# Identity matmuls in planned idle stretches of TensorE: a hybrid recurrent backbone on one core

## The chip, the cores and the metric

The kernel runs on 1 core of one Trainium2 chip, in one launch. The metric is device time in microseconds (us) of the whole program. PE is TensorE, DVE is VectorE, ACT is ScalarE, POOL is GpSimd, SP is SyncE, which here issues the DMAs.

## The reference

Four layers of one trunk over 512 tokens (256 context, 256 latent) of width 1024, in float32. Each layer mixes tokens by two parallel recurrences and then applies a gated feed-forward:

```
hg, rw, gt = split(modulate(rms_norm(x)) @ w_in[l])        # 1024 -> 6528 columns
o_hg = hgrn2_branch(hg)      # 4 heads, gated linear recurrence, both directions
o_rw = rwkv7_branch(rw)      # 8 heads, S = S*w + sa b^T + v k^T, both directions
m = sigmoid(g_hg) * (o_hg @ proj_a) + sigmoid(g_rw) * (o_rw @ proj_b)
x = x + gate * rms_norm(m @ w_out)
x = x + gate2 * rms_norm((silu(gt) * up) @ w2)             # hidden width 2816
```

The shifts, scales and gates come from a conditioning vector through `ada_w` (6144 columns a layer). The recurrences of the latent tokens start from the final states of the context. In the last layer the context gives only those states.

## The kernel before

Activations stand transposed, 128 channels by 512 tokens a tile. Each large product is made of three matmuls on high and low parts of weights and activations: a weight block lands in `wr`, ACT copies its high part to `wh`, DVE or POOL subtracts to get `wl`, and PE adds `wl*hh`, `wh*hh` and `wh*hl` into a PSUM bank `p_ps`. Small products use the banks `s_ps`, `g_ps` and `c_ps`.

The RWKV branch runs as four pairs of heads, in chunks of 64 tokens. `rw_pair` prepares a pair, `rw_solve` inverts small triangles on DVE (tiles `XS`, `S`), and `rw_chain` walks over 8 chunks with its products in one bank, `c_ps`. A step of the walk goes over the engines in turn: 4 matmuls `c_ps<-UV,SC`; ACT copies the result to `S`; 4 matmuls with the inverse; ACT copies to `UV`; 4 matmuls `c_ps<-UV,BKT`; then 6 updates on DVE, 4 of `UV` and 2 of `S`, each of which reads `c_ps`; then the next step.

No instruction is issued where the source calls it. All calls are recorded as nodes of a graph (`Plan.add`), `Plan.schedule` puts them in an order for each engine by assumed costs, ranks and lags between engines, and `Plan.emit` issues them in the order of the planned times. The plan has its own picture of PE's clock: in stretches that it believes slow it doubles PE's costs, and what it believes changes the order of real work. When the calls are issued, the framework adds the semaphore waits that reads and writes of a tile need, for the tile as a whole.

The first work of the program is `ada_first`: 32 matmuls of `ada_w` rows into `g_ps`, as the DMAs land, in two groups of 16; then four transposes by the identity `ident`; beside them the first norm (squares on ACT into `fn`, of which there are three buffers, summed on PE by `ones` into `s_ps`). `ident` is loaded by a DMA that the plan puts 25th on SP's queue.

Of the kernel before, what the change touches and what calls it, by code (L numbers as in the profile page):

```python
# [2 lines left out]

# [6 lines left out]
F32 = mybir.dt.float32  # L10
F32R = mybir.dt.float32r
U8 = mybir.dt.uint8
AF = mybir.ActivationFunctionType
# [3 lines left out]
P = 128  # L17
# [12 lines left out]
C = 64  # L30
# [40 lines left out]
        ('pe', True): 30, ('act', True): 0, ('vec', True): 30, ('pool', True): 0, ('dma', True): 0}  # L71
MAXLOOK = 200
WINDOW, COLD = 4096 / 1.2, (0.39, 0.87)


def bias_of(bias, kind):
    return bias[kind[1]].get(kind[0], 0.0) if kind else 0.0


def isc(kind):  # L80
    return kind is not None and kind[0] == "C"


class Node:
# [4 lines left out]
    def __init__(self, engs, calls, preds, costs, load, kind):  # L89
        self.engs, self.calls, self.preds, self.costs, self.load, self.kind = engs, calls, preds, costs, load, kind  # L90


class Plan:
# [4 lines left out]

    def __init__(self, nc, tc):
        self.tc, self.nodes, self.tiles, self.tags, self.gang, self.kind = tc, [], {}, {}, None, None  # L100
        self.share = 1.0
        self.eng = dict(zip(self.ENG, (nc.tensor, nc.scalar, nc.vector, nc.gpsimd, nc.sync)))
        for name in self.ENG:
            setattr(self, name, Recorder(self, (name,)))
        self.any = Recorder(self, ("vec", "pool"))
# [137 lines left out]
    def schedule(self):  # L243
        nodes = self.nodes
        N = len(nodes)
        succ = [[] for _ in range(N)]
        need = [0] * N
        for i, x in enumerate(nodes):
            need[i] = len(x.preds)
            for p in x.preds:  # L250
                succ[p].append(i)
        rank = [0.0] * N
        for i in range(N - 1, -1, -1):
            x = nodes[i]
            lag = self.LAG.get(x.engs[0])
            m = 0.0
            for s in succ[i]:
                v = rank[s] + (lag[nodes[s].engs[0]] if lag else DMA_LAG + x.load)
                if v > m:
                    m = v  # L260
            rank[i] = m + x.costs[0]
        rank = [r + bias_of(BIAS, x.kind) for r, x in zip(rank, nodes)]
        ready = {e: [] for e in self.ENG}
        later = {e: [] for e in self.ENG}
        free = {e: 0.0 for e in self.ENG}
        when = [0.0] * N
        on = [None] * N
        bus = 0.0
        edge, busy, cold = WINDOW, 0.0, True
        tail = 1e9  # L270

        def release(i):
            for e in nodes[i].engs:
                heapq.heappush(later[e], (when[i], i))

        for i in range(N):
            if not need[i]:
                release(i)
        order = []
        while len(order) < N:  # L280
            best = None
            for e in self.ENG:
                while ready[e] and on[ready[e][0][1]]:
                    heapq.heappop(ready[e])
                while later[e] and on[later[e][0][1]]:
                    heapq.heappop(later[e])
                if ready[e]:
                    t = free[e]
                elif later[e]:
                    t = max(free[e], later[e][0][0])  # L290
                else:
                    continue
                if best is None or t < best[0]:
                    best = (t, e)
            t, e = best
            while later[e] and later[e][0][0] <= t:
                _, i = heapq.heappop(later[e])
                if not on[i]:
                    heapq.heappush(ready[e], (-rank[i], i))
            if ready[e] and later[e] and later[e][0][0] <= t + MAXLOOK:  # L300
                r0 = -ready[e][0][0]
                m = min((x for x in later[e] if x[0] <= t + MAXLOOK and rank[x[1]] > r0 + 2000.0 and not on[x[1]]
                         and x[0] <= t + LOOK[e, isc(nodes[x[1]].kind)]), default=None)
                if m is not None and m[0] + 1e-6 < t + nodes[ready[e][0][1]].costs[0]:
                    free[e] = m[0]
                    continue
            _, i = heapq.heappop(ready[e])
            x = nodes[i]
            on[i] = e
            c = x.costs[x.engs.index(e)]  # L310
            if e == "pe":
                if t <= free[e]:
                    c += max(0.0, x.head - tail)
                tail = x.tail
                while t >= edge:
                    cold = busy < (COLD[1] if cold else COLD[0]) * WINDOW
                    busy = max(0.0, free[e] - edge) if free[e] > edge else 0.0
                    edge += WINDOW
                if cold:
                    c *= 2.0  # L320
                busy += (min(t + c, edge) - t) * x.load
            end = t + c
            free[e] = end
            order.append((t, i))
            if e == "dma":
                bus = max(bus, t) + x.load
            for s in succ[i]:
                r = bus + DMA_LAG if e == "dma" else end + self.LAG[e][nodes[s].engs[0]]
                if r > when[s]:
                    when[s] = r  # L330
                need[s] -= 1
                if not need[s]:
                    release(s)
        order.sort()
        self.when, self.on = order, on
        return max(free.values())
# [17 lines left out]
def body(ctx, tc, xT, cc, ada_w, w_in, rw_lo, rw_g2, proj_a, proj_b, w_out, ffn_w1, ffn_w2,  # L354
         vecs, lbl, c_id, c_bo, c_sc, c_hg, c_sh, out, depth=4):
    nc = tc.nc
    plan = Plan(nc, tc)
    vec, act, pool, pe, dma = plan.vec, plan.act, plan.pool, plan.pe, plan.dma
# [6 lines left out]
    pss = ctx.enter_context(tc.tile_pool(name="pss", bufs=1, space=PSUM))  # L365
# [9 lines left out]
    def const(ap, dt=F32, name=None):  # L375
        t = plan.tile(cst, list(ap.shape), dt, None, 1, name)
        dma.dma_start(t, ap)
        return t

    ident = const(c_id, name="ident")  # L380
# [14 lines left out]
    vec.memset(onef, 1.0)  # L395
    vec.tensor_copy(ones, onef)

    def sps(tag="s"):
        return plan.tile(pss, [P, 512], F32, tag, PSB[tag], tag + "_ps")

    hgf = st("SS", [P, 6, C])
# [119 lines left out]
    def proj(src, nk, c0, xh, xl, t0, place=None):  # L521

        ps = sps("p")
        if place:
            ws = weights(src, nk, c0, place)
            for c, a, b in halves(t0):
                for k, (wh, wl) in enumerate(ws):
                    mm3(ps[:, a:b], wh, wl, xh[k][:, a:b], xl[k][:, a:b], k == 0, k == nk - 1)
            return ps
        for k0 in range(0, nk, KB):  # L530
            n = min(KB, nk - k0)
            wh, wl = load_split(src, k0, n, c0, P)
            for k in range(n):
                kk = k0 + k
                mm3(ps[:, t0:T], wh[:, k, :], wl[:, k, :], xh[kk][:, t0:T], xl[kk][:, t0:T],
                    kk == 0, kk == nk - 1)
        return ps
# [204 lines left out]
    hd = (slice(0, C), slice(C, P))  # L742

    def layer(l, pm, xs, xd, hh, hl):
        last = l == depth - 1
# [285 lines left out]
        def rw_chain(p):  # L1031
# [12 lines left out]
            for s in range(NCH):  # L1044
                ps = sps("c")
# [53 lines left out]
                with plan.together(0.75):  # L1099
                    for x in steps:  # L1100
                        st_, i, d, n = x
                        for h in range(2):
                            po = ps[hd[h], 384 + i * C:384 + (i + 1) * C]
                            if st_:
                                w, a = S[hd[h], d, n % 4, :], ARt[hd[h], d, n, 1, :]
                            else:
                                w, a = UV[:, d, n, h, :], SC[:, d, n, h, C:P]
                            pe.matmul(po, w, a[:, ::-1] if d else a, start=x == steps[0], stop=fin[i] == x,
                                      skip_group_check=True)
                st_ = ns[1] - ns[0]  # L1110
                act.activation(y.rearrange("p (n c) -> p n c", c=C)[:, ns[0]:ns[1] + 1:st_],
                               ps[:, 384:512].rearrange("p (n c) -> p n c", c=C), AF.Copy)
                flags["chain", p] = s
                yield 1

# [2 lines left out]
            ps = sps()  # L1118
# [6 lines left out]
            ps = sps()  # L1125
# [7 lines left out]
            ps = sps()  # L1133
# [184 lines left out]
        while run:  # L1318
# [8 lines left out]
            try:  # L1327
                x = next(r[3])
# [99 lines left out]
        if not last:  # L1428
            ada_to(l + 1, 2)
        h = norms(xs, t0, (pr[:, 5], lambda j: proj(ffn_w2[l], NF, j * P, gh, gl, t0),  # L1430
                           tail(ffn_w2[l], NF, gh, gl, spot), NK if last else NK - NTL[1]),
                  None if last else (pms[l + 1]["pr"][:, 0], pms[l + 1]["pr"][:, 1]))
# [31 lines left out]
    h = norms(xs, 0, pre=(pms[0]["pr"][:, 0], pms[0]["pr"][:, 1]))  # L1464
    for l in range(depth):
        ada["end"] = l + 1
        xs, xd, h = layer(l, pms[l], xs, xd, *h)
# [57 lines left out]
```

## Time and profile before

| what | value |
|---|---|
| median of 3 runs | 4313.35 us (4310.06 to 4324.89) |
| profiled execution, its own time | 4312.55 us |
| its span, first to last instruction | 4310.8 us |
| PE busy | 3855.0 us, 89% |
| DVE busy | 3309.3 us, 77% |
| ACT busy | 2149.9 us, 50% |
| mean granted clock of PE | 0.932 of 2.4 GHz |

The granted clock takes two levels, 1.2 and 2.4 GHz; a mean of a stretch says how much of it was at either. Idle before an instruction is idle time of its engine, with what ended it. A float32 matmul stands in the trace as two passes, so 4 matmuls are 8 rows there; a transpose is one.

### The profile page before, as it was taken

The page shows a single profiled execution, that of the slowest core. Times are in us where ns is not written, and L with a number is a line of the kernel's source. Part 1 is how long each engine was busy: PE and PEld are TensorE (multiplying, and loading weights), DVE is VectorE, ACT ScalarE, POOL GpSimd, SP SyncE. Part 2 cuts the span into 40 slices and gives each one's busy share as a digit, 9 for nine tenths or more (in the row PEclk, how much of TensorE's full clock was granted, in tenths as well). Part 3 has the DMA queues.
Part 4 walks back from the last instruction along what each step waited for, and adds up shares of the span by engine and source line. Part 5 has one row for each costly group of instructions (what it writes and reads, how often), then busy time and mean ns, then how long its engine had stood idle before and what let it go on. Part 6 is the DMA issues. An engine that isn't in the chain of part 4 may idle for free.

```text
span 4310.8 us, 71511 instructions
## 1 busy us (share of the span) xinstructions
PE 3855.0 (89%) x26290; PEld 3058.9 (71%) x26290; DVE 3309.3 (77%) x5764; ACT 2149.9 (50%) x4234; POOL 1890.7 (44%) x1617
## 2 busy tenths in 40 slices
PE   7889998899988998999999889899899997788898
PEld 4666666777776666677777766677777775567798
DVE  5989979999179899668753898987676379988676
ACT  4556653433255566544333555565433255566564
POOL 1343444455433444464554243454455433244332
PEclk8889899999998898999999989899999998788999
DMA  4111137466321111363543212116354331112555
GB/s 150 57 53 48 52 122 217 138 182 177 91 85 52 59 50 55 122 186 115 159 123 107 64 38 63 43 56 221 108 164 140 108 102 45 41 51 63 170 151 160
DMA packets 661407, 451.02 MB, mean 105 GB/s; under 512 B 28224, under 2 KB 584256, under 8 KB 661056
## 3 DMA queue, kind: packets, MB, share of 16 engines
q1 hardware_dynamic: 661056, 446.44, 34.7%
q8 instruction: 207, 3.39, 0.3%
q14 instruction: 144, 1.18, 0.1%
HBM read 416.98 MB, written 29.36 MB: 104 GB/s over the span
## 4 chain that ended last, share of the span: by engine, by line
PE 42%; DVE 19%; issue 10%; POOL 5%; ACT 2%; DMA 1%; POOLq 0%; SPq 0%; DVEq 0%; ACTq 0%
PE p_ps L343 32%; POOL wl L343 4%; PE s_ps L343 4%; DVE XS L343 4%; PE c_ps L343 3%; PE g_ps L343 2%; DVE wl L343 2%; DVE S L343 2%; DVE X8b L343 1%; DVE AR L343 1%; DVE hX L343 1%; DVE UV L343 1%; DVE X8a L343 1%; DVE BK L343 1%; DVE X4c L343 1%
## 5 line engine op out<-in xcount | busy, mean ns | idle before, releaser
L343 PE MATMUL p_ps<-hh,wl 128*128 128x512 f32 (+1 forms) x2784 | 1091.0, 397 | 107.0 <-DVE wl L343 53.5
L343 PE MATMUL p_ps<-hh,wh 128*128 128x512 f32 (+1 forms) x2784 | 1073.9, 390 | 0.0
L343 PE MATMUL p_ps<-hl,wh 128*128 128x512 f32 (+1 forms) x2784 | 1066.2, 389 | 0.0
L343 ACT ACTIVATE wh<-wr 128x512 fp32r<-128x512 f32 x986 | 611.0, 622 | 860.8 <-PE p_ps L343 684.4
L343 POOL TENSOR_TENSOR wl<-wr,wh 128x512 fp32r<-128x512 f32 x487 | 674.3, 1392 | 746.9 <-ACT wh L343 517.0
L343 PEld LDWEIGHTS p_ps<-hh,wl 128*128 128x128 f32 x2784 | 543.7, 196 | 245.9 <-POOL wl L343 77.0
L343 PEld LDWEIGHTS p_ps<-hl,wh 128*128 128x128 f32 x2784 | 541.8, 195 | 97.6 <-issue 7.2
L343 PEld LDWEIGHTS p_ps<-hh,wh 128*128 128x128 f32 x2784 | 543.6, 196 | 90.7 <-issue 4.9
L343 DVE TENSOR_TENSOR wl<-wr,wh 128x512 fp32r<-128x512 f32 (+1 forms) x499 | 377.6, 762 | 99.6 <-ACT wh L343 89.9
L343 POOL TENSOR_SCALAR fn<-fn 128x512 f32<-128x512 f32 (+1 forms) x152 | 236.4, 1555 | 246.1 <-ACT fn L343 220.0
L343 POOL TENSOR_SCALAR S0P<-S,pcs 128x64 f32<-128x64 f32 x192 | 151.4, 802 | 316.8 <-DVE S L343 316.2
L343 DVE TENSOR_TENSOR fn<-fn,p_ps 128x512 f32<-128x512 f32 (+1 forms) x208 | 127.7, 615 | 162.0 <-ACT fn L343 81.2
L343 ACT ACTIVATE fn<-fn 128x512 f32<-128x512 f32 (+1 forms) x304 | 174.5, 575 | 103.2 <-POOL fn L343 98.8
L343 POOL TENSOR_TENSOR HB<-HB,HA 128x512 f32<-128x512 f32 x112 | 157.7, 1408 | 155.2 <-ACT hY L343 153.2
L343 DVE TENSOR_TENSOR XS<-XS,S 64x30 f32<-64x30 f32 (+14 forms) x480 | 203.9, 425 | 11.7
L343 DVE TENSOR_TENSOR S<-XS 64x30 f32<-64x30 f32 (+14 forms) x480 | 193.2, 402 | 11.6
L343 POOL COPY SC<-XS 64x256 f32<-64x256 f32 x128 | 67.6, 528 | 263.1 <-DVE SC L343 250.3
L343 POOL TENSOR_TENSOR HA<-HA 128x512 f32<-128x512 f32 x112 | 144.2, 1287 | 11.4 <-ACT hX L343 5.0
L343 PE MATMUL p_ps<-SC,wh 128*128 128x512 f32 (+1 forms) x440 | 144.2, 361 | 0.0
L343 DVE SCALAR_TENSOR_TENSOR UV<-c_ps,pcs,S0P 64x64 f32<-64x64 f32 x384 | 108.6, 283 | 36.7 <-PE c_ps L343 26.6
L343 ACT ACTIVATE fn<-p_ps 128x512 f32<-128x512 f32 (+1 forms) x217 | 112.2, 518 | 42.9 <-PE p_ps L343 23.6
L343 ACT ACTIVATE hY<-HB 128x512 f32<-128x512 f32 x128 | 85.0, 664 | 89.2 <-PE g_ps L343 74.5
(478 smaller groups left out, 8761.7 us busy)
## 6 DMA issues: line engine op xcount, KB each, us to landing
wr<-ffn_w SPq DMA_DIRECT2D x512, 256.0 KB, 3.1
wr<-w_in SPq DMA_DIRECT2D x408, 256.0 KB, 2.9
hq<-ada_w SPq DMA_DIRECT2D x242, 256.0 KB, 3.0
PB<-ada_w SPq DMA_DIRECT2D x110, 256.0 KB, 2.8
wr<-w_out SPq DMA_DIRECT2D x64, 256.0 KB, 3.0
gts<-fn SPq DMA_DIRECT2D x48, 256.0 KB, 2.4
wr<-proj_a SPq DMA_DIRECT2D x32, 256.0 KB, 3.9
wr<-proj_b SPq DMA_DIRECT2D x32, 256.0 KB, 3.6
```

The source lines that it names most:

```text
L343: getattr(self.eng[self.on[i]], name)(*args, **kw)
```

## The change

A chain's bank `c_ps` was a new tile in each step; it is now one tile, `cbank`, for the whole program. The outputs of the chain that stood in its columns 384 to 511 move to 128 to 255. The freed columns take filler matmuls, identity times identity, 128x128 in float32. They are put in by `schedule`: where PE's next node would start at least 300 ns after PE is free, and the plan's running measure of PE's use is under 0.85, fillers of assumed 216 ns are placed from the free time on, as long as 300 ns are left. Their time counts in the plan's picture of the clock. The fillers are not nodes with predecessors or successors. The first may be placed once the plan has issued (not landed) the DMA of `ident`.

```
+FILL, FMIN, FUSE = 216.0, 300.0, 0.85
...
+                f = free[e]
+                while f >= since and t - f >= FMIN and use < FUSE:
+                    turn(f)
+                    d = 2.0 * FILL if cold else FILL
+                    nodes.append(Node(("pe",), [self.filler], set(), [FILL], 1.0, None))
+                    on.append("pe")
+                    order.append((f, len(nodes) - 1))
+                    fills += 1
+                    spent(f, d, 1.0)
+                    f += d
+                turn(t)
...
+            if i == self.needs:
+                since = end
...
+    cbank = plan.tile(pss, [P, 512], F32, None, 1, "c_ps")
+    plan.filler = ("matmul", (cbank[:, 384:512], ident, ident), dict(start=True, stop=True))
+    plan.needs = plan.tiles[ident.tensor.name][0][0][0]
...
-                            po = ps[hd[h], 384 + i * C:384 + (i + 1) * C]
+                            po = ps[hd[h], 128 + i * C:128 + (i + 1) * C]
```

The built program has 297 fillers in 78 places: 31 before the first `p_ps` matmul, 93 in the rest of the first three layers, and 173 in the last layer. The order of real work changes too: taking the fillers out, 12388 of 20460 matmul rows of PE stand at the same position; the rest, all four layers' mixing stages among it, is rearranged, and the feed-forward stages are mostly as they were.

The first place is PE's start, before. `g_ps<-SC,ep` are the first matmuls of `ada_first`; the names in brackets are the semaphores an instruction waits for, `DMAHW0` to `DMAHW7` those of DMAs in turn.

```order
L343 MATMUL g_ps<-SC,ep 32x512 [waits DMAHW4_49]
L343 MATMUL g_ps<-SC,ep 32x512 [waits DMAHW5_49]
L343 MATMUL g_ps<-SC,ep 32x512 [waits DMAHW6_49]
L343 MATMUL g_ps<-SC,ep 32x512 [waits DMAHW7_49]
L343 MATMUL g_ps<-SC,ep 32x512 [waits DMAHW0_49]
...
L343 MATMUL g_ps<-BKT,ep 32x512 [waits DMAHW1_49]
L343 MATMUL s_ps<-fn,ones 128x256 [waits Activation_49] x2
L343 MATMUL g_ps<-UV,ep 32x512 [waits DMAHW1_49]
```

The same stretch of PE after the change.

```order
L373 MATMUL g_ps<-SC,ep 32x512 [waits DMAHW4_49]
L373 MATMUL c_ps<-ident 128x128 [waits DMAHW6_49]
L373 MATMUL g_ps<-SC,ep 32x512 [waits DMAHW5_49]
L373 MATMUL g_ps<-SC,ep 32x512
L373 MATMUL g_ps<-SC,ep 32x512 [waits DMAHW7_49]
...
L373 MATMUL c_ps<-ident 128x128 x2
...
L373 MATMUL c_ps<-ident 128x128 x12
L373 MATMUL s_ps<-fn,ones 128x256 [waits Activation_49] x2
L373 MATMUL c_ps<-ident 128x128 x13
L373 MATMUL g_ps<-UV,ep 32x512 [waits DMAHW1_49]
```

A filler now stands fifth on PE and waits for the DMA of `ident`; the two later matmuls whose data come by earlier DMAs of the same semaphore need no wait of their own any more. 27 further fillers stand between it and the second group of `g_ps`. SP's first 41 rows are as they were.

The second place is the first step of the third chain in the last layer, on PE, before.

```order
L343 MATMUL s_ps<-wd_5213,BK 128x512 [waits PE_49]
L343 MATMUL c_ps<-UV,BKT 64x64 [waits Activation_49]
L343 MATMUL c_ps<-UV,BKT 64x64 x3
L343 MATMUL s_ps<-ad_5219,BK 128x512 [waits PE_49]
L343 MATMUL s_ps<-wd_5213,BK 128x512
L343 MATMUL s_ps<-ad_5219,BK 128x512
L343 MATMUL c_ps<-UV,SC 64x64 [waits DVE_49,PE_49]
```

The same step on PE after.

```order
L373 MATMUL s_ps<-ad_5124,BK 128x512
L373 MATMUL c_ps<-UV,BKT 64x64 [waits Activation_49]
L373 MATMUL c_ps<-UV,BKT 64x64 x3
L373 MATMUL c_ps<-ident 128x128 x2
L373 MATMUL c_ps<-ident 128x128 [waits DVE_49] x6
L373 MATMUL c_ps<-UV,SC 64x64 x4
```

Eight fillers stand between the two products of the chain, and six of them each wait for a DVE instruction.

The third place is DVE's updates in that step, before.

```order
L343 TENSOR_TENSOR hX<-hX,og 128x256 [waits DVE_49]
L343 TENSOR_SCALAR UV<-c_ps,pcs 64x64 [waits PE_49,Activation_49]
L343 TENSOR_SCALAR UV<-c_ps,pcs 64x64 x3
L343 TENSOR_SCALAR S<-c_ps,pcs 128x64 x2
L343 TENSOR_TENSOR X8b<-X8a 64x8x64 [waits Activation_49]
```

The same updates after.

```order
L373 TENSOR_TENSOR X8a<-X8a,X8b 128x512
L373 TENSOR_SCALAR UV<-c_ps,pcs 64x64 [waits PE_49,Activation_49]
L373 TENSOR_SCALAR UV<-c_ps,pcs 64x64 [waits PE_49] x3
L373 TENSOR_SCALAR S<-c_ps,pcs 128x64 [waits PE_49] x2
L373 TENSOR_TENSOR X8b<-X8a 64x8x64 [waits DVE_49]
```

Before, the first update waits for PE and the other five follow it. After, each of the six waits for PE: a filler writes the tile that the updates read, so the filler waits for the update before it, and the update behind it waits for the filler. Over the whole program 25 DVE updates, all in the last layer, wait in this way for a filler that itself waits for a DVE update; 8 other DVE updates and 12 ACT copies wait for a run of fillers (45 in all) that follows the matmuls they read; and the other 15 fillers that wait for ACT (11) or DVE (4) stand ahead of further real work of the chain.

## Rows read from the trace of the kernel before

**Rows 1.** The cores' view: span and mean granted clock.

```profile
core 0: 4310.8 us, clock 0.932
```

**Rows 2.** The page's chain that ended last: share of the span by engine.

```profile
PE 42%; DVE 19%; issue 10%; POOL 5%; ACT 2%; DMA 1%; POOLq 0%; SPq 0%; DVEq 0%; ACTq 0%
```

**Rows 3.** Timeline of PE, 4 to 59 us: start, us, instruction, [idle before <-releaser].

```profile
4.86 7.08 PE L343 MATMUL g_ps<-SC,ep 128*32 128x512 f32 x16 [4.86 <-DVE ep L343]
14.48 3.04 PE L343 MATMUL g_ps<-BKT,ep 128*32 128x512 f32 x8
22.86 2.07 PE L343 MATMUL s_ps<-fn,ones 128*128 128x256 f32 x4 [5.34 <-ACT fn L343]
35.04 2.56 PE L343 MATMUL g_ps<-UV,ep 128*32 128x512 f32 x4 [10.11 <-DMA UV<-ada_w]
...
38.52 0.62 PE L343 MATMUL g_ps<-X8a,ep 128*32 128x512 f32 x2
...
40.77 1.36 PE L343 MATMUL g_ps<-X4c,ep 128*32 128x512 f32 x4
49.21 1.11 PE L343 MATMUL g_ps<-ident,fn 128*128 128x128 f32 x4 [7.07 <-ACT fn L343]
...
58.02 0.50 PE L343 MATMUL p_ps<-hh,BKT 128*128 128x256 f32 x2 [1.98 <-ACT hh L343]
```

**Rows 4.** SP's issue of `ident`, and DMA issues: count, size, us to landing.

```profile
25.16 0.33 SPq L343 DMA_DIRECT2D ident<-c_id  x1
ident<-c_id SPq DMA_DIRECT2D x1, 64.0 KB, 4.4
```

**Rows 5.** Timeline of ACT, 24 to 49 us.

```profile
24.12 0.42 ACT L343 ACTIVATE fn<-XS 128x256 f32<-128x256 f32 x1 [0.70 <-PE s_ps L343]
30.76 0.63 ACT L343 ACTIVATE SC<-wr 128x512 fp32r<-128x512 f32 x1 [6.22 <-DMA wr<-w_in]
...
48.57 0.58 ACT L343 ACTIVATE fn<-g_ps 128x512 f32<-128x512 f32 x1
```

**Rows 6.** Windows of mixing in the last three layers, and two inside the last.

```profile
core 0: us, PE busy (x) PEld busy (x) DVE busy (x) ACT busy (x) POOL busy (x), PEclk, DMA share, GB/s
1235.00:1816.00 581.00, 516.78 (x4296) 392.34 (x4295) 508.82 (x976) 333.82 (x670) 237.63 (x228) 0.90 0.20 60
2376.00:2943.00 567.00, 505.25 (x4272) 383.12 (x4271) 494.19 (x971) 330.83 (x666) 229.19 (x225) 0.92 0.19 57
3505.00:4023.00 518.00, 435.15 (x3837) 350.06 (x3836) 460.50 (x938) 306.90 (x665) 215.42 (x225) 0.87 0.20 59
3720.00:3780.00 60.00, 38.76 (x373) 31.62 (x374) 54.81 (x112) 26.09 (x52) 14.09 (x19) 0.63 0.10 29
3860.00:3900.00 40.00, 26.71 (x259) 21.78 (x260) 37.09 (x81) 16.23 (x37) 12.77 (x21) 0.64 0.08 24
```

**Rows 7.** Chain that ended last in 3505 to 4023 us, by line.

```profile
by line: PE p_ps L343 22.2%; DVE XS L343 9.2%; PE s_ps L343 7.9%; PE c_ps L343 6.5%; issue 6.4%; DVE wl L343 6.1%; DVE S L343 5.8%; DVE AR L343 4.8%; DVE X8b L343 3.9%; PE g_ps L343 3.4%; DVE UV L343 2.9%; DVE hX L343 2.4%; DVE X8a L343 2.3
```

**Rows 8.** Timeline of PE and DVE, third chain's first step in the last layer.

```profile
3862.29 0.45 PE L343 MATMUL c_ps<-UV,BKT 128*64 128x64 f32 x8
3862.86 1.18 DVE L343 TENSOR_SCALAR UV<-c_ps,pcs 64x64 f32<-64x64 f32 x4 [1.12 <-PE c_ps L343]
3864.05 0.48 DVE L343 TENSOR_SCALAR S<-c_ps,pcs 128x64 f32<-128x64 f32 x2
3864.68 0.65 PE L343 MATMUL c_ps<-UV,SC 128*64 128x64 f32 x8 [0.85 <-DVE S L343]
```

**Rows 9.** 128x128 matmuls by the identity: tile's view (min/median/max ns), groups by form.

```profile
L343 PE MATMUL g_ps<-ident,fn x4: 421/421/475, 49.2 to 49.9; 128*128 128x128 f32 x4
L343 PE MATMUL s_ps<-ident,BK 128*128 128x128 f32 x128 | 21.0, 286 | 5.6 <-DVE SC L343 5.5
```

**Rows 10.** DVE's reads of `c_ps`, whole program: idle time before them, by what ended it.

```profile
  PE c_ps L343: 33.2, 35
```

More of the change, by code (lines that the diff above doesn't have):

```diff
@@ L1 @@
 import heapq
+import math
 from contextlib import ExitStack, contextmanager
@@ L100, in __init__ @@
         self.tc, self.nodes, self.tiles, self.tags, self.gang, self.kind = tc, [], {}, {}, None, None
-        self.share = 1.0
+        self.share, self.filler, self.needs = 1.0, None, None
         self.eng = dict(zip(self.ENG, (nc.tensor, nc.scalar, nc.vector, nc.gpsimd, nc.sync)))
@@ L270, in schedule, with turn, spent @@
         tail = 1e9
+        use, last, fills, since = 0.0, 0.0, 0, 1e18
+        def turn(t):
+            nonlocal edge, busy, cold, use, last
+            while t >= edge:
+                cold = busy < (COLD[1] if cold else COLD[0]) * WINDOW
+                busy = max(0.0, last - edge) if last > edge else 0.0
+                edge += WINDOW
+            if t > last:
+                use *= math.exp((last - t) / WINDOW)
+                last = t
+        def spent(t, c, load):
+            nonlocal busy, use, last
+            busy += (min(t + c, edge) - t) * load
+            w = math.exp(-c / WINDOW)
+            use = use * w + load * (1.0 - w)
+            last = t + c
         def release(i):
@@ L279, in schedule @@
         order = []
-        while len(order) < N:
+        while len(order) < N + fills:
             best = None
@@ L314, in schedule @@
                 tail = x.tail
[L315 to L318, printed above, removed]
+                f = free[e]
[9 more added lines that the diff above has]
+                turn(t)
                 if cold:
                     c *= 2.0
-                busy += (min(t + c, edge) - t) * x.load
+                spent(t, c, x.load)
             end = t + c
@@ L396, in body @@
     vec.tensor_copy(ones, onef)
+    cbank = plan.tile(pss, [P, 512], F32, None, 1, "c_ps")
+    plan.filler = ("matmul", (cbank[:, 384:512], ident, ident), dict(start=True, stop=True))
+    plan.needs = plan.tiles[ident.tensor.name][0][0][0]
     def sps(tag="s"):
+        if tag == "c":
+            return cbank
         return plan.tile(pss, [P, 512], F32, tag, PSB[tag], tag + "_ps")
@@ L1111, in rw_chain @@
                 act.activation(y.rearrange("p (n c) -> p n c", c=C)[:, ns[0]:ns[1] + 1:st_],
-                               ps[:, 384:512].rearrange("p (n c) -> p n c", c=C), AF.Copy)
+                               ps[:, 128:256].rearrange("p (n c) -> p n c", c=C), AF.Copy)
                 flags["chain", p] = s
```

## The prediction

> **What bounds the kernel now.** I read the cores' view first: a span of 4310.8 us at a mean granted clock of 0.932 [rows 1]. With two levels, 1.0 and 0.5, that is (1 - 0.932) / 0.5 = 13.6% of the span at the lower one, some 586 us. The chain that ended last lies 42% on PE and 19% on DVE [rows 2]. If the slow time were spread evenly over the chain's PE work, a full clock throughout would give back at most 0.42 x 586 / 2 = 123 us. So the clock is worth something; the question is what 297 fillers reach of it, and what they hold up.
>
> Next I read the windows. In the last layer's mixing, 3505 to 4023 us, DVE is busy 460.5 of 518 us and PE 435.2, at a mean clock of 0.87; in the two slowest stretches, 3720 to 3780 and 3860 to 3900, the clock is 0.63 and 0.64, PE is busy 38.8 of 60 and 26.7 of 40 us, but DVE 54.8 and 37.1 [rows 6]. DVE sets the pace there, and PE is slow because it is waiting. The chain by line says the same: in that mixing PE's four PSUM lines hold 22.2 + 7.9 + 6.5 + 3.4 = 40%, DVE's lines most of the rest [rows 7]. Of the fillers, 173 of 297 stand in this layer, and 31 at the start of the program. I work out these two places and bound the rest.
>
> **The start.** In the trace the first g_ps matmuls run from 4.9 us as their data land, and the first group ends near 17.5 us [rows 3]. After the change the fifth instruction on PE waits for ident, which SP issues at 25.16 us and which lands 4.4 us later, at 29.6 us [rows 4]. SP's order ahead of it is unchanged and waits for nothing on PE, so that landing stays. PE stands from some 8 us to 29.6 us. Then it has to run what it had done before: 12 matmuls of g_ps, 24 passes. A pass costs 0.139 us where nothing holds it (26 passes from 38.52 to 42.13 us [rows 3]), so 3.3 us. With them stand 28 fillers; a pass of 128 columns at the lower clock comes every (1.11 - 0.42) / 3 = 0.23 us [rows 3, 9], a filler is two, so 0.46 us, or 0.23 us at the full clock: 6.4 us. The norm's two matmuls take 2.07 us at the lower clock [rows 3], about 1 us at the full one. Together 10.7 us at the full clock. PE has been idle, so I let the first 4.5 us run at half speed (before, PE ran slowly from 35.04 to about 38.5 us [rows 3]): 29.6 + 10.7 + 2.25 = 42.6 us, where the second group of g_ps began at 35.04; its 32 passes, now unhindered, take 4.5 us and end at 47.1 us instead of 42.1: 5 us late.
>
> The other path is ACT's. Its fourth square, at 24.12 us, waits for the first norm matmul on PE to free a buffer [rows 5]; that matmul now comes at about 39 us. Behind the square in ACT's queue stand the weight copies that began at 30.76 us and, as the last of them all, the copy of g_ps at 48.57 us [rows 5]. They start near 39.5 us, 8.8 us late. Some waits of theirs for DMAs shrink, since the data have landed meanwhile; I take 2 to 3 us off, which leaves 6 to 7. The transposes that begin at 49.21 us [rows 3], and everything after them, wait for that copy. I take +6.5 us, with ends of +4 (all of ACT's lag recovered but PE's part) and +9 (none recovered). Nothing later can hide it: the whole first layer hangs on this norm.
>
> **The chain of the last layer.** Before, the 4 + 2 updates of a step run back to back on DVE, 1.18 + 0.48 us, and the next matmul starts 0.15 us after the last (3864.53 to 3864.68 us); the first starts 0.12 us after PE's matmuls end (3862.74 to 3862.86 us) [rows 8]. With a filler between two updates DVE pays, for each, 0.15 us to PE, one filler, and 0.12 us back. No filler is in the trace; the nearest rows are the identity matmuls of one pass, 0.286 us at mostly full clock and 0.421 at the lower [rows 9], to which the second pass adds 0.115 or 0.23. So a round trip is 0.27 + 0.40 = 0.67 us, or 0.27 + 0.65 = 0.92. There are 25: 17 to 23 us. I take 0.75 us each, 19 us. Queued behind the waiting update are all of DVE's other instructions, and DVE is the engine that is 89% busy in this mixing, so no cover is left; the lower end is still 5 us, if many updates stand where DVE would have waited for PE anyhow. In the trace DVE waited for c_ps 35 times, 33.2 us in all, in the 112 steps of the program [rows 10].
>
> By the same rows a third of the readers that wait for a run of fillers would be there in time to feel it: 20 readers, 2.25 fillers each, 0.23 to 0.46 us a filler; 20 / 3 x 2.25 x 0.3 = +4 us, ends 0 and +20. The 15 other fillers that wait and have real work behind them cost about 0.3 us each: +4 us, ends 0 and +7. Fillers that wait for nothing, some 220 after the start, cost 0 where PE is idle as planned, and 0.23 us where it is not; at 42% of the chain that is at most 220 x 0.23 x 0.42 = 21 us. Many stand at layer starts, where PE waits for the norm; I take +3.
>
> **The clock.** In the last layer's mixing the lower level holds (1 - 0.87) / 0.5 = 26% of 518 us, 135 us [rows 6]. With 40% of the chain on PE, all of it returned is 135 x 0.40 / 2 = 27 us. The fillers cover parts of it, and what PE gains where DVE is late goes to waiting. I take -10 us, ends 0 and -27. The start's fillers return nothing, since PE falls idle again before the transposes.
>
> The Trainium skill speaks on both sides (TensorE: Matmul & The Clock Gate). Its section on why this matters for kernels wants PE kept free of idle gaps between bursts of matmuls, as the filler does; by that alone the sum would be the second rival below. The note on the warm-up in its Part 1, on the HAM clock gate, puts the ramp's penalty below 1% of a typical span; an estimate by that page is at most 43 us here, and the trace, at 0.932, does not agree that it is so little [rows 1].
>
> **Order.** Real work is rearranged in all four mixing stages. How much an order is worth can be bounded by two stages that hold the same work in different orders: 581 and 567 us in the second and third layer [rows 6], 14 us apart. I take 0, with ends of -14 and +20 over the four.
>
> **The sum.** +6.5 + 19 + 4 + 4 + 3 - 10 = +26.5 us on the execution's own 4312.55 us: 4339 us. That execution is 0.8 us under the median of 4313.35, so the base is the same within the scatter.
>
> **The rivals.**
> Hidden: the round trips fall where DVE waits anyhow, and the clock returns little. What is left is the start: 4312.55 + 6.5 = 4319 us, no change that can be told. For it speaks that DVE's order has changed around the updates, and that DVE already waits for c_ps in a third of its steps [rows 10]; against it, DVE's 460.5 busy us of 518.
> The clock returns: the fillers keep PE at 2.4 GHz through the last mixing, and the round trips cost only their lower end: 4312.55 + 6.5 + 5 + 3 - 27 = 4300 us, and with an order that is 5 us better 4295, faster. For it speaks that the slow stretches are where PE is least busy, and that most fillers are there; against it, that in them DVE is the later one [rows 6]. It wins from the point where the clock gives back more than the waits take, about 28 us.
> The order decides: the tuned arrangement is lost in all four stages at the upper end of 20 us, on top of the forecast: 4359 us, slower.
> Fillers that change nothing on the chip are not a rival by themselves: the wait for ident alone is in the program.
>
> **How the numbers follow.** Forecast 0.55, hidden 0.22, clock 0.14, order 0.09. A measurement here can tell about 0.3%, 13 us: slower is above 4326, faster below 4300. Of the forecast a tenth falls short of 4326; of hidden a fifth lies above it by its order and a tenth below 4300; of the clock case four fifths are faster, the rest the same; the order case is slower. So slower is 0.495 + 0.045 + 0.09 = 0.63, faster 0.02 + 0.11 = 0.13, and 0.24 remains for the same. The likeliest case alone has 4322 to 4362 us from the ends of its terms; the range that leaves out no more than 2 in 10 is 4301 to 4368.
>
> **What would show it.** Right: PE idle from about 8 to 29.6 us in front of c_ps<-ident, the first p_ps matmul some 6 us later than 58.0 us [rows 3]; in the last layer DVE's updates of UV and S apart by about 1 us instead of 0.30, each released by PE c_ps, and DVE's idle time before reads of c_ps 20 us above 33.2. Wrong: the last mixing shorter than 518 us with a clock well over 0.87, or updates apart but DVE no later, which makes it hidden; or feed-forward stages that change length, which nothing here explains.

## The result, and the profile after

The changed kernel takes 4392.49 us, the median of 4 runs (4384.08 to 4407.85), against 4316.68 of the kernel before beside it: a ratio of 1.0169 [1.0149, 1.0190], some 73 us slower. Slower was forecast, but at 4339 us, and the range ended at 4368.

The cores' view after, against [rows 1]:

```profile
core 0: 4390.6 us, clock 0.931
```

The mean clock is what it was. The start, PE's timeline (columns as in [rows 3]) and ACT's under it, against [rows 3, 5]:

```profile
4.87 3.70 PE L373 MATMUL g_ps<-SC,ep 128*32 128x512 f32 x8 [4.87 <-DVE ep L373]
29.27 0.80 PE L373 MATMUL c_ps<-ident 128*128 128x128 f32 x2 [20.70 <-DMA ident<-c_id]
30.00 1.94 PE L373 MATMUL g_ps<-SC,ep 128*32 128x512 f32 x8
...
38.55 1.03 PE L373 MATMUL s_ps<-fn,ones 128*128 128x256 f32 x4
39.41 3.06 PE L373 MATMUL c_ps<-ident 128*128 128x128 f32 x26
42.41 1.07 PE L373 MATMUL g_ps<-UV,ep 128*32 128x512 f32 x8
...
55.32 1.11 PE L373 MATMUL g_ps<-ident,fn 128*128 128x128 f32 x4 [9.27 <-ACT fn L373]
...
62.93 0.50 PE L373 MATMUL p_ps<-hh,BKT 128*128 128x256 f32 x2 [1.98 <-ACT hh L373]
```

```profile
39.18 0.42 ACT L373 ACTIVATE fn<-XS 128x256 f32<-128x256 f32 x1 [16.24 <-PE s_ps L373]
...
54.69 0.58 ACT L373 ACTIVATE fn<-g_ps 128x512 f32<-128x512 f32 x1
```

PE stands for 20.7 us until `ident` lands, ACT's fourth square follows PE's norm matmul, the copy of `g_ps` comes 6.1 us later than before, and the first `p_ps` matmul 4.9 us later.

The last layer's mixing and its third chain, by windows (columns as in [rows 6]). Here and below "the last mixing" runs from the first `hh<-fn` of that layer to the `XS<-x` of its output product; in the kernel before that is 3493.2 to 4022.8 us, 529.6 us, which is a little wider than the window of [rows 6]. Its row before:

```profile
3493.20:4022.80 529.60, 445.10 (x3889) 359.34 (x3890) 470.67 (x961) 313.61 (x681) 217.70 (x228) 0.87 0.20 59
```

The third chain before:

```profile
3862.90:3976.20 113.30, 93.37 (x889) 75.48 (x888) 100.66 (x206) 68.03 (x150) 52.32 (x53) 0.84 0.17 51
```

The third chain and the last mixing after:

```profile
3904.00:4047.80 143.80, 121.53 (x985) 99.78 (x985) 101.19 (x204) 60.63 (x137) 41.84 (x46) 0.80 0.13 36
...
3510.90:4092.50 581.60, 505.34 (x4173) 413.18 (x4174) 471.66 (x948) 307.76 (x666) 209.91 (x227) 0.85 0.18 52
```

The last mixing is 52 us longer, though DVE's busy time is 1 us more. PE, fillers included, is busy 60 us longer, and the clock is no higher. The third chain takes 143.8 us instead of 113.3. The chain that ended last, by line, in the last mixing, against [rows 7]:

```profile
by line: PE p_ps L373 21.0%; PE c_ps L373 16.6%; PE s_ps L373 9.9%; DVE XS L373 7.5%; DVE S L373 6.4%; issue 5.5%; DVE wl L373 5.0%; DVE AR L373 3.2%; DVE UV L373 2.8%; DVE X8b L373 2.7%; PE g_ps L373 2.6%; DVE hX L373 1.9%; DVE X8a L373 1.
```

PE's `c_ps` lines held 6.5% of 518 us before, 34 us; now they, with the fillers among them, hold 16.6% of 581.6 us, 97 us. That is where the time of this stage is. The first step of the third chain, DVE and then PE, against [rows 8]:

```profile
3904.01 0.28 DVE L373 TENSOR_SCALAR UV<-c_ps,pcs 64x64 f32<-64x64 f32 x1 [1.13 <-PE c_ps L373]
3904.87 0.29 DVE L373 TENSOR_SCALAR UV<-c_ps,pcs 64x64 f32<-64x64 f32 x1 [0.58 <-PE c_ps L373]
...
3908.34 0.28 DVE L373 TENSOR_SCALAR S<-c_ps,pcs 128x64 f32<-128x64 f32 x1 [0.58 <-PE c_ps L373]
```

```profile
3904.34 0.49 PE L373 MATMUL c_ps<-ident 128*128 128x128 f32 x2 [0.44 <-DVE UV L373]
3905.22 0.49 PE L373 MATMUL c_ps<-ident 128*128 128x128 f32 x2 [0.39 <-DVE UV L373]
...
3908.68 0.52 PE L373 MATMUL c_ps<-ident 128*128 128x128 f32 x2 [0.38 <-DVE S L373]
```

The updates now start 0.87 us apart instead of 0.30: each behind the first waits 0.58 us for a filler, which waited for the update before it. Six updates took 1.67 us; now they take 4.6.

A later step of the same chain, PE and then ACT, shows the other kind of wait:

```profile
3934.13 1.12 PE L373 MATMUL c_ps<-UV,SC 128*64 128x64 f32 x8
3935.17 1.22 PE L373 MATMUL c_ps<-ident 128*128 128x128 f32 x4
3936.86 0.79 PE L373 MATMUL c_ps<-ident 128*128 128x128 f32 x2 [0.47 <-ACT S L373]
3937.59 0.69 PE L373 MATMUL c_ps<-S,AR 64*64 64x64 f32 x8
```

```profile
3936.43 0.38 ACT L373 ACTIVATE S<-c_ps 64x256 f32<-64x256 f32 x1 [8.47 <-PE c_ps L373]
```

The chain's matmuls end near 3935.25 us, but ACT's copy of them starts at 3936.43: two fillers hold it for 1.2 us. A third, behind the copy, holds the next product for 0.73 us more.

The tile's views: the idle time that PE's `c_ps` ended before reads by DVE (before: [rows 10]) and by ACT:

```profile
  PE c_ps L373: 71.6, 65
...
  PE c_ps L373: 287.7, 168
```

### The profile page after: what moved, and what is told of

Same layout as the page of the kernel before. It is cut to its first block, busy times and chain, and to the rows that moved or that the text cites. A ratio compares the mean times of both kernels' runs of the same rounds, so it can differ in the third digit from the quotient of the medians.

```text
span 4390.6 us, 72652 instructions
## 1 busy us (share of the span) xinstructions
PE 3936.8 (90%) x26884; PEld 3137.9 (71%) x26884; DVE 3312.4 (75%) x5762; ACT 2146.8 (49%) x4234; POOL 1868.5 (43%) x1619
## 4 chain that ended last, share of the span: by engine, by line
PE 38%; DVE 16%; issue 6%; POOL 3%; ACT 2%; DMA 1%; DVEq 0%; POOLq 0%; ACTq 0%
PE p_ps L373 28%; PE c_ps L373 4%; PE s_ps L373 4%; POOL wl L373 3%; DVE XS L373 3%; DVE S L373 2%; PE g_ps L373 2%; DVE wl L373 2%; DVE AR L373 1%; DVE X8b L373 1%; DVE UV L373 1%; DVE hX L373 1%; DVE X8a L373 1%; DVE X4c L373 1%; ACT wh L373 0%
## 5 line engine op out<-in xcount | busy, mean ns | idle before, releaser
L373 POOL TENSOR_SCALAR S0P<-S,pcs 128x64 f32<-128x64 f32 x192 | 135.0, 716 | 361.1 <-DVE S L373 357.8
L373 DVE TENSOR_TENSOR S<-XS 64x30 f32<-64x30 f32 (+14 forms) x480 | 208.2, 434 | 12.2
L373 PE MATMUL c_ps<-ident 128*128 128x128 f32 x594 | 116.0, 337 | 38.8 <-DMA ident<-c_id 20.7
L373 ACT ACTIVATE fn<-p_ps 128x512 f32<-128x512 f32 (+1 forms) x217 | 112.3, 518 | 48.8 <-PE p_ps L373 26.5
```

Source lines behind the costliest of these rows:

```text
L373: getattr(self.eng[self.on[i]], name)(*args, **kw)
```

## The experiments

Each ran beside the kernel before on the same chip, whose median was 4314.9 to 4321.9 us there; comparisons go by ratios. Two kernels are set against each other through their ratios to before, and such a difference is good to about 0.3%. In per cent of 4316.7 us, 0.1% is 4.3 us, so 0.3% is 13 us. Stages and idle times are read from one profiled execution of each kernel, which lies up to 11 us from its median.

**The order alone.** In `emit`:

```
 for _, i in self.when:
+    if self.nodes[i].calls[0] is self.filler:
+        continue
```

> The plan of the changed kernel with the fillers counted in the plan but none of the 297 issued: its order of real work alone. Theory F (the fillers cost, by holding PE and the readers of the chain's bank in the last layer): 4315 to 4335 us, most of the 76 us gone, the last layer's mixing (first norm to the load of XS) back from 582 to 530-540 us. Theory O (the new order costs): 4360 to 4390 us, the last mixing still over 565 us.

Measured 4347.05 us, 1.0068 [1.0046, 1.0090]: 29 us slower than before without one filler. The last mixing and the two idle times (DVE, ACT) before reads of `c_ps`:

```profile
3510.70:4048.60 537.90, 449.04 (x3848) 363.90 (x3849) 471.34 (x948) 308.44 (x667) 214.31 (x227) 0.84 0.19 56
```

```profile
  PE c_ps L375: 34.7, 37
...
  PE c_ps L375: 232.6, 162
```

The first theory had 4315 to 4335 us for this run and the second 4360 to 4390: neither came. DVE's idle time before its reads of the chain is about what it was, 33.2 us, so the loss is not there. 8 us are in the last mixing and as much in the stretch behind it, 288.0 us before and 295.7 here. Two stretches between mixing and feed-forward, with the output product and the norm, lose about as much: 132.8 us became 141.2 in the second layer, and the first layer's rows stand below, before and then here. The rest is spread.

```profile
636.10:796.90 160.80, 132.43 (x572) 98.50 (x572) 142.29 (x189) 57.38 (x107) 80.22 (x53) 0.95 0.69 211
633.70:801.50 167.80, 139.34 (x586) 103.54 (x584) 146.09 (x191) 58.81 (x108) 80.08 (x56) 0.92 0.68 209
```

This run also keeps the one tile `cbank` and the moved columns. No run has these in before's order without fillers, so what they cost by themselves is not shown. That they change the waits is: PE's weight loads (PEld) for `c_ps` wait for a DVE read 85 times here and 38 times before. Before, then here:

```profile
  PEld c_ps L343: 26.2, 38
...
  PEld c_ps L375: 82.6, 85
```

**The fillers alone.** The plan keeps a second state of the clock that fillers don't enter, and costs go by that one, so every engine has before's order of real work; 221 fillers find a place.

```
+while t >= edge1:
+    cold1 = busy1 < (COLD[1] if cold1 else COLD[0]) * WINDOW
+    ...
...
-if cold:
+if cold1:
     c *= 2.0
```

> The other half: every engine's real work in the order of the kernel before, with 221 fillers put in by the same rule from a second copy of the plan's clock that does not touch the order. It has 16 DVE updates or more in the last layer that wait for a filler, and the wait for ident at the start. Theory F: 4350 to 4375 us, the last mixing 25 to 45 us longer than before's 529.6. Theory O: 4317 to 4330 us, the start's 5 us and little else.

Measured 4346.47 us, 1.0063 [1.0040, 1.0087], between the ranges of both theories. The last mixing takes 544.2 us here (3508.5 to 4052.7), 15 us longer than before's 529.6, where the first theory wanted 25 to 45. So each half by itself is some 28 us slower; the fillers' half has 221 here and 297 in the change, and it has the one tile too.

**No round trips.** The 27 fillers between two reads of one step are left out.

```
...
+elif p is not None and nxt[i] is not None and self.on[p] != "pe" and self.on[nxt[i]] != "pe":
+    drop.add(i)
...
```

> The changed kernel without the 27 fillers that stand between two reads of the chain's bank in one step: no DVE or ACT read waits for a filler that waits for a read; 270 fillers stay. If the round trips are what cost (theory F, waits): some 25 x 0.6 to 0.9 us = 15 to 23 us off, 4370 to 4378 us. If PE's time for the fillers is what costs (theory F, occupancy): under 10 us off, above 4382. Theory O: the same as the changed kernel, 4385 to 4395 us.

Measured 4369.59 us, 1.0109 [1.0079, 1.0138]: 0.60% or 26 us below the changed kernel. The idle time before reads of `c_ps` falls from 71.6 us on DVE and 287.7 us on ACT to

```profile
  PE c_ps L396: 50.8, 41
...
  PE c_ps L396: 269.5, 167
```

ACT's falls by 18 us although 25 of the 27 fillers stand between reads of DVE, so the idle time before a read also holds what delays the chain ahead of it.

**No fillers beside the chain.** The 93 fillers that stand next to a chain matmul on PE are left out, the round trips among them; 204 stay.

```
...
+        if nxt is not None and cb(nxt):
+            drop.add(i)
...
+        if prev is not None and cb(prev):
+            drop.add(i)
...
```

> The changed kernel without the 93 fillers next to a matmul of the chain's bank on PE; 204 fillers stay, those between other work and at the start. Theory F: 4330 to 4350 us (the chain's share of the cost is most of it). If the fillers beside other work cost as much for each one: 4365 to 4375. Theory O: 4380 to 4392 us.

Measured 4338.94 us, 1.0047 [1.0024, 1.0070]: 1.22% or 53 us below the changed kernel, and 0.21% below the order alone, which is not clear of noise. The last mixing:

```profile
3511.00:4042.90 531.90, 451.14 (x4002) 370.26 (x4003) 472.52 (x948) 308.33 (x667) 214.93 (x229) 0.89 0.19 57
```

50 of the 53 us come back in this one stage, and its clock is now 0.89. With the fillers beside the chain it was 0.85, and with no filler at all, in the run of the order alone, 0.84: filling that chain did not raise the clock there.

**No fillers ahead of a reader.** As the one without round trips, but `self.on[p] == "pe"`: the 61 fillers between a chain matmul and the DVE or ACT read behind it are left out.

> The changed kernel without the 61 fillers that stand between a matmul of the chain and the DVE or ACT read of its bank behind it; 236 stay, the round trips among them. Of the 61, 45 are ahead of a reader that waits for them. The prediction's term for these readers was 4 us (a third of them in time to feel it, 0.3 us a filler): 4385 to 4390 by that. Theory now (every reader is on time, and a filler costs the 0.49 to 0.64 us that it takes with its weight load): 45 x 0.5 = 20 to 25 us below the changed kernel, 4367 to 4372.

Measured 4374.29 us, 1.0115 [1.0090, 1.0140]: 0.54% or 23 us below the changed kernel. The two idle times, DVE and ACT:

```profile
  PE c_ps L396: 61.8, 63
...
  PE c_ps L396: 268.9, 169
```

Both fall, by 10 and 19 us, ACT's as much as without the round trips, so ACT's idle time does not tell the two apart. Round trips and held readers, each left out by itself, add up to 49 of the 53 us by the ratios. The last mixing of the two profiled executions, without round trips and without these fillers, says less:

```profile
3514.10:4078.30 564.20, 491.46 (x4121) 404.40 (x4122) 470.84 (x948) 308.02 (x667) 211.96 (x227) 0.85 0.18 53
```

```profile
3512.40:4078.30 565.90, 485.88 (x4064) 393.96 (x4065) 472.75 (x949) 308.10 (x667) 212.68 (x229) 0.85 0.18 54
```

They give back 17 and 16 us there, of the 50 that come back without all 93. No run leaves out both and nothing else, so the other 17 are not settled; the clock, 0.85 in these two and 0.89 there, may be part of them.

**Shorter fillers beside the chain.** The 93 compute 32 columns.

```
...
+if i in few:
+    args = (args[0][:, :32], args[1], args[2][:, :32])
...
```

> The changed kernel with all its 297 fillers in the same places and with the same waits, but the 93 that stand next to a matmul of the chain on PE compute 32 columns instead of 128. Theory (what the 66 of them outside the round trips cost, some 30 us, is their own time on PE, 0.45 us each, on the chain that is the critical path; of a round trip's 0.85 us it is half): 66 x 0.3 + 27 x 0.25 = 20 to 27 us below the changed kernel, 4365 to 4373. Rival (the cost is the crossing between engines, whatever the filler's length): at most 8 us below it, above 4384.

Measured 4391.82 us, 1.0175 [1.0158, 1.0192]: nothing gained; the theory failed, and the time is in the rival's range. PE in the same step as above:

```profile
3909.91 0.41 PE L395 MATMUL c_ps<-ident 128*128 128x32 f32 x2 [0.37 <-DVE UV L395]
3910.71 0.57 PE L395 MATMUL c_ps<-ident 128*128 128x32 f32 x2 [0.38 <-DVE UV L395]
3911.66 0.64 PE L395 MATMUL c_ps<-ident 128*128 128x32 f32 x2 [0.38 <-DVE S L395]
```

A quarter of the columns takes 0.41 us instead of 0.49 at 2.4 GHz, and here the clock falls to the lower level within the step, where it takes 0.64. So the run doesn't separate a filler's time from its waits as intended: the time hardly changed. The Trainium skill (TensorE: Matmul & The Clock Gate, section on LDWEIGHTS) says that a weight load goes by the columns of the weights; the trace agrees so far that the two loads of a filler take 0.30 us in either kernel at 2.4 GHz, the changed one first:

```profile
3905.22 0.30 PEld L373 LDWEIGHTS c_ps<-ident 128*128 128x128 f32 x2 [0.58 <-DVE UV L373]
```

```profile
3909.91 0.30 PEld L395 LDWEIGHTS c_ps<-ident 128*128 128x128 f32 x2 [0.48 <-DVE UV L395]
```

**A bank of their own.** Three runs with `p=3` in `PSB`, which frees a bank; the plan comes out anew, the same for all three.

```
-PSB = dict(p=4, s=2, c=1, g=1)
+PSB = dict(p=3, s=2, c=1, g=1)
...
+fbank = plan.tile(pss, [P, 512], F32, None, 1, "f_ps")       # second run only
-plan.filler = ("matmul", (cbank[:, 384:512], ident, ident), ...)
+plan.filler = ("matmul", (fbank[:, 384:512], ident, ident), ...)
```

The fillers in the chain's bank:

> The changed kernel with three banks p_ps instead of four, fillers in the chain's bank as in the change. The plan comes out anew with it: 344 fillers, of which 82 stand next to a matmul of the chain and 20 between two reads of one step. It is the partner of the two runs beside it, which have the same order of real work; by itself it says only what a bank less costs. By the theory that waits through the shared bank cost 0.85 us a round trip and about 0.45 us a filler elsewhere beside the chain, it is 20 x 0.85 + 62 x 0.45, some 45 us less 10 us of clock, above the run without fillers. Rival (the loss is the order's and the fillers' mere presence on PE): within 10 us of the run with a bank of their own.

In their own:

> Every engine's order as in the run with three banks p_ps and shared bank, the 344 fillers at the same places, but they write to the bank that became free, which nobody reads. No filler waits for DVE or ACT and no reader waits for a filler. Theory (the waits through the shared bank are the loss): 25 to 45 us faster than its partner with the shared bank, and 0 to 15 us faster than its partner without fillers, since the clock's gain remains and only 0.49 us of PE time for a filler that is late. Rival (the fillers' time on PE ahead of the chain's matmuls is the loss): at most 10 us faster than the shared bank, and above the partner without fillers.

Without them:

> The same order of real work with three banks p_ps, and none of the 344 fillers issued: the base of the two runs beside it. Where the shared bank's waits are the loss, it stands 30 to 40 us below the shared bank and at or a little above the bank of their own; where fillers cost only their time on PE, it is the fastest of the three.

Measured 4429.51 us, 1.0241 [1.0218, 1.0264], shared; 4395.78 us, 1.0169 [1.0150, 1.0188], own; 4388.93 us, 1.0151 [1.0126, 1.0177], none. DVE's idle time before reads of `c_ps`, one row from each, in this order:

```profile
  PE c_ps L373: 68.3, 59
```

```profile
  PE c_ps L373: 49.1, 38
```

```profile
  PE c_ps L375: 48.2, 37
```

The same fillers at the same places cost 0.72%, 31 us, more when they share the chain's bank, so sharing the bank costs by itself. But this is another plan, with 20 round trips, and its loss lies elsewhere: from the first `hh` to the last mixing, shared and own, it is 26 of the 32 us between the two profiled executions.

```profile
62.20:3585.70 3523.50, 3196.03 (x20686) 2498.56 (x20686) 2631.99 (x4426) 1668.75 (x3210) 1566.72 (x1313) 0.94 0.34 101
```

```profile
63.30:3560.50 3497.20, 3177.32 (x20686) 2488.54 (x20686) 2626.36 (x4426) 1669.26 (x3209) 1568.70 (x1313) 0.95 0.34 102
```

The last mixing gives back 5 us of them: 551.8 us shared, 546.8 own. What the waits cost in the changed kernel's last mixing has to be read from the runs in its own order. The other half of the theory missed: in a bank of their own the fillers don't win against none (0.18% or 8 us above, within the intervals). The start can account for that: the first filler waits for `ident` in either bank, and the first `hh` comes at 63.3 us with fillers, at 56.2 without. The last mixing, shared, with a bank of their own, and without fillers:

```profile
3585.70:4137.50 551.80, 476.08 (x4098) 387.78 (x4099) 463.16 (x955) 311.58 (x672) 216.90 (x228) 0.88 0.19 55
```

```profile
3560.50:4107.30 546.80, 476.43 (x4098) 390.40 (x4098) 463.15 (x956) 311.79 (x672) 219.62 (x228) 0.88 0.19 56
```

```profile
3541.20:4088.70 547.50, 449.97 (x3858) 362.71 (x3858) 463.96 (x955) 311.94 (x672) 219.36 (x228) 0.84 0.19 55
```

From none to own the clock rises from 0.84 to 0.88 and the stage is 0.7 us shorter; DVE is busy 463 and 464 us of it. The Trainium skill (Perfetto Trace Analysis, section on optimizing Tensor performance) wants independent groups of matmuls in different banks, so that their readers overlap with the next group; these three runs agree, in that readers of the chain's bank wait 19 us longer on DVE when the fillers share it.

**The best of both.** Before's order, and 150 fillers: none ahead of the first `p_ps` matmul, none beside the chain.

```
...
+elif not begun or (prev is not None and cb(prev)):
+    drop.add(i)
...
```

> The order of real work of before on every engine, and 150 fillers: none before the first p_ps matmul, and none that stands next to a matmul of the chain on PE. Theory (three separate terms: order about +27 us, fillers next to the chain about +50, all other fillers -8 with the start's +5 in them): the first two terms and the start are gone, so 8 to 13 us below before, with less time at the lower clock than in the run of the order alone (614 us): about 540. Rival (the fillers' clock gain belongs to the new order, or PE is not on the path where the clock comes back): within 4 us of before, whatever the clock. Second rival (fillers that wait for nothing still delay real work): 5 to 15 us above before.

Measured 4323.26 us, 1.0013 [1.0002, 1.0023], 12 runs: the theory failed. It is 5.6 us slower than before, with an interval of 0.9 to 9.9, though the time at the lower clock, summed over the trace, fell from 584 to 556 us. That lies in the second rival's range (fillers that wait for nothing still delay real work, 5 to 15 us), and the first rival's 4 us can't be excluded. The one tile is in this run as well, so the 5.6 us need not be the fillers'. No version here beats the kernel before.

**Other orders.** The kernel before, one constant of its plan changed; no filler anywhere.

```
-WINDOW, COLD = 4096 / 1.2, (0.39, 0.87)
+WINDOW, COLD = 3900 / 1.2, (0.39, 0.87)      # first run
+WINDOW, COLD = 4096 / 1.2, (0.35, 0.83)      # second run
```

> The kernel before, without fillers and without the shared bank; one constant of the plan's picture of the clock, its window, is 5% shorter. The plan rearranges about as much as the change did (11551 of 20460 PE rows at the same position, against 12412). Theory (the order of before is a selected one, and any rearrangement by the plan loses part of it): 10 to 40 us above before. Rival (the change's order is worse because its picture counts fillers, which is a worse picture): a 5% shorter window is nearly the old picture, so within 8 us of before, on either side.

> The kernel before, without fillers; both thresholds of the plan's picture of the clock are 0.04 lower (0.35 and 0.83), so that it believes PE fast a little more often, as counted fillers make it believe. 13212 of 20460 PE rows at the same position. Theory (any rearrangement loses part of a selected order): 10 to 40 us above before, like the other constant. Rival (a worse picture costs, a nearly equal one does not): within 8 us of before.

Measured 4348.99 us, 1.0077 [1.0063, 1.0091], and 4330.42 us, 1.0030 [1.0019, 1.0042]: 33 and 13 us slower. The last mixing of each:

```profile
3510.30:4054.00 543.70, 449.56 (x3884) 364.19 (x3884) 463.06 (x958) 314.34 (x679) 217.66 (x229) 0.86 0.19 56
```

```profile
3494.30:4038.50 544.20, 456.79 (x3884) 371.63 (x3885) 459.64 (x958) 314.43 (x680) 215.09 (x228) 0.84 0.19 56
```

Both lose 14 to 15 us there with the work unchanged. A small push to what the plan believes costs 13 to 33 us, about the size of the change's own order with the one tile, 29.

## Why the prediction was wrong

The direction was right, and the start and the round trips came near their prices; the forecast of +26.5 us was 46 us short of the 73 us. By ratios: the order with the one tile +29, the fillers away from the chain and at the start together -9, the round trips +26, the held readers +23, and +4 left of the 53 us beside the chain. Each is good to about 13 us, so the -9 and the +4 are not clear of zero. By the last mixing of the profiled executions the two kinds of wait are 17 and 16 us, and 17 of the 50 stay open.

**The order failed first.** The step "I take 0, with ends of -14 and +20" took two stages of one order as a sample of orders. It is +29, with whatever the one tile adds, for which the prediction had no term. Three rearrangements, each by a different edit of the plan's picture of the clock, all lose: 0.68, 0.77 and 0.30%; the last two have no filler and no shared tile. The two layers that lie 14 us apart belong to one arrangement; how far another falls was nowhere in the trace of before. That before's order is a selected one is the reading that fits; which moved instruction costs what stays open. By the profiled executions of the run of the order alone, 17 of 34 us are in the first three layers, and 15 of these 17 between mixing and feed-forward in the first two.

**The held readers failed by size.** The step "a third of the readers that wait for a run of fillers would be there in time to feel it", at 0.3 us a filler, gave 4 us. It is 23 by the ratios and 16 by the last mixing. From the order alone to the changed kernel, the idle time before reads of `c_ps` grows by 36.9 us on DVE and 55.1 us on ACT. How much of that is the readers' own wait the idle time doesn't say, since the round trips are in it; the run without these fillers does. By an estimate from a filler's measured 0.49 to 0.79 us, the 45 that hold a reader cost 22 to 36 us if every reader feels them and 7 to 12 if a third does; 16 to 23 lies above the third. And a filler alone costs 0.49 us at 2.4 GHz and 0.79 at 1.2; I had taken the interval between passes that follow each other without a gap, 0.23 to 0.46. The upper end that I had written down, 20 us, was near it.

**The round trips held.** 19 us predicted for 25; 26 us measured for 27 fillers, within the error, and 17 in the last mixing. DVE's idle time falls by 20.8 us without them. "20 us above 33.2" had been asked for, and it stands 38.4 above: the held readers are in it too. The pitch of 0.87 against 0.30 us is 0.57 us each at 2.4 GHz, a little under the 0.67 that I had put together from its parts.

**The start held.** +4.9 us at the first `p_ps` matmul for 6.5 predicted; `ident` was there at 29.27 us for 29.6, the fourth square ran at 39.18 for 39, and the copy of `g_ps` came 6.1 us late. ACT recovered more behind it than I took off. Without the start's fillers the first `hh` comes at 57.4 us, as before (57.5).

**The clock failed in its place.** The -10 us were to come from the last layer's mixing. There the clock was 0.84 in the order alone, 0.89 with only the fillers away from the chain, and 0.85 with all of them. Why those beside the chain cost clock is not shown: that each made an engine wait, and PE with it, would fit, but with three banks `p_ps` the stage is at 0.88 whether the fillers share the chain's bank or not. Fillers away from the chain did cut the slow work: PE's real work at the lower level (its busy time outside the fillers, in the stretches of lower granted clock, summed over the trace) goes from 478 to 394 us between the order alone and the run without fillers beside the chain, and half of the difference, 42 us, is PE time saved. The kernel got 9 us faster, or 14 with the start's loss set apart, neither clear of the 13 us. In before's order the cut is from 463 to 438 us and nothing comes of it, nor with a bank of their own (497 to 442 us). So no run shows a gain from the clock that is clear of noise, and 14 us is the most that any suggests; the windows of [rows 6], with DVE busier than PE, had pointed that way.

**The cases.** The rival in which the order decides had the right mechanism and 0.09 of the chance, but its 4359 us held only 20 us of order on top of the forecast. The range failed because the upper ends of order (+20) and readers (+20) were treated as if they would not come together; with both, and the clock at 0, the sum's own ends give 4312.55 + 6.5 + 19 + 20 + 4 + 3 + 20 = 4385 us.

## What to carry to other kernels

An instruction that is put in to keep an engine busy needs an output that nobody waits for: the same fillers cost 31 us more in the chain's bank than in one of their own. Where a planner makes the order, an edit that shifts its costs can pay for the new order too, so run that order without the edit's work first, and the edit's other parts, here the one tile, without the new order. And a higher clock need not be worth anything: 0.84 to 0.88 gave 0.7 us of 547 in a stage where DVE was busy 463.

## What was not expected of the hardware

A 128x128 float32 filler that stands alone takes 0.49 us at 2.4 GHz and 0.79 at 1.2, and with a quarter of the columns still 0.41 and 0.64. So most of the price does not go by the columns; the rows of its two weight loads, at 2.4 GHz, span 0.30 us in both. Matmuls put into a chain that waits at every step need not hold the clock up: in the third chain of the last layer PE was busy 121.5 of 143.8 us and the granted clock was 0.80, against 93.4 of 113.3 us and 0.84 before. In the order alone this chain's clock is 0.78 (3886.8 to 4003.9 us).
